# A scan's input products with their three precision parts stacked along the contraction, and its matrices laid out on the host

## The chip, the cores and the metric

The kernel runs on one core of one Trainium2 chip. The time is device microseconds of that core, from runs of the compiled program; a profiled execution of the same program gives the trace. TensorE (PE, with its weight loads as PEld), VectorE (DVE), ScalarE (ACT) and GpSimd (POOL) each take their instructions in program order and wait for each other through semaphores; SP's queue and POOL's queue issue the DMA transfers.

## The reference, cut to what matters

One decoder layer for 304 tokens (16 meta, 256 prompt, 32 sample): a SwiGLU block, a mixer and a second SwiGLU block, in float32. The mixer projects its input to a pooled branch, a state-space branch and two gates. The state-space branch is the part that is changed:

```python
b_bar = ((lam_bar - 1.0) / lam)[..., None] * b_mat          # (64 groups, 64 states, 16 channels), complex
ug = u.astype(f32).reshape(nb, L, N_SSM_GROUPS, SSM_GS)     # 64 groups of 16 channels
bu = jnp.einsum('blgc,gpc->blgp', ug.astype(jnp.complex64), b_bar)
...
_, h = lax.associative_scan(combine, (a, bu), axis=1)       # h[t] = lam_bar * h[t-1] + bu[t]
y = jnp.einsum('blgp,gcp->blgc', h, c_mat).real
```

So each group of 16 channels is multiplied by its own 64 x 16 complex matrix, the states run along the tokens, and each group is multiplied back.

## The kernel before, in words

**Projections.** Channels lie on partitions, tokens along the free dimension. A weight comes in chunks of 4 x 128 rows by 256 columns (512 KB), loaded by SP's queue three chunks deep. Every float32 product is made of three float32r ones: ACT rounds the chunk to its high part (`whi`, line 158), DVE makes the rest (`wlo`, line 167), and `mm3` (lines 245 to 247) multiplies high by high, high by low and low by high into one PSUM bank: 24 matmuls per chunk. `whi` and `wlo` have four buffers each. `step` (after each chunk) sets the order of all the rest: it casts the chunk three ahead, runs what the last projection left to do (`g.post`), makes the low part, starts a load, and then advances a side generator by `g.rate` turns; a turn is what lies between two `yield`s. `SETRATE` is 1.25 turns per chunk while the scan's tables are made, `MIXRATE` 2.25 while the scan runs. Nothing is reordered later: an instruction that waits holds back all that follows it on its engine.

**The setup** (`ssm_setup`, side work of the first SwiGLU block) makes the scan's tables. Of it the change touches the input matrices: b (states on partitions) is multiplied by two tables of coefficients `cr` and `ci` (lines 785 to 793) into the real part, the imaginary part and their sum, `bx[0..2]`; for each of 8 blocks `spread` copies the pieces into a block-diagonal tile (ACT), PE transposes it three times (`bt`, line 831), ACT and DVE split it into high and low part (`bc`, lines 832 and 833), and POOL's queue writes it to DRAM (`bsc`, line 835).

**The scan** (`Scan`) goes through 8 blocks of 128 channels. A block has four quads of 32 channels (two groups each), and each quad gives 128 state rows. `parted` (lines 877 and 878) splits the block's input `u` into `uhi` and `ulo`. `into`, once for each `ri` (sum, imaginary, real), multiplies: four quads times three part products, 12 matmuls of 32 contraction rows each (line 888), where the quads lie on different partitions; ACT copies the four banks into `row` tiles (line 892). Then `rows` turns half a block at a time (two quads, 12 turns): products with the tables `ee`, subtractions, two first-order scans (line 924), products back, and the states (line 943). `outof` (line 903) multiplies the rows by the c matrices, three turns into the next block. POOL's queue loads `ee` (line 860), the b matrices `bs` (line 867) and the c matrices `cs` (line 870).

**Around it.** While the scan runs, PE does the rest of the mixer's projections: the last part of the input projection, the pooled branch's map (`pw`, two chunks, each split into `Y` by ACT and DVE, line 274, which also frees its PSUM bank), then gates and branch products (`pj`). The main PSUM pool has four banks, the auxiliary one three, and one bank is apart.

Of the kernel before, what the change touches and what calls it, by code (L numbers as in the profile page):

```python
# [18 lines left out]
P = 128  # L19
# [22 lines left out]
NJ = 32  # L42
JB = 2
NA = S0 // 16
NTV = 16 + NA
POOLRATE = 3.5
LATE = 8
STIR = 9
LAG = 2
ROWS = 15  # L50
MAGIC = 12582912.0
# [6 lines left out]
def host_consts():  # L58
    import numpy as np

    c = np.zeros((P, NT + NTV), np.float32)
    c[:, :NT] = 1.0
    c[:, 0] = 0.0
    c[:, S0:NT:NS] = 0.0
    c[:, NT:NT + 16] = np.arange(16)
    c[:, NT + 16:NT + NTV] = 16 * np.arange(NA)
    return {"consts": c}

# [132 lines left out]
def tables(g):  # L201
    g.ident = g.const.tile([P, P], F32, name="ident")
    make_identity(g.nc, g.ident)
    g.hc = g.const.tile([P, NT + NTV], F32, name="hc")
    g.nc.gpsimd.dma_start(g.hc, g.I["consts"])
# [50 lines left out]
def bank(g, name, aux=False, pool=None):  # L256
    return (pool or (g.psaux if aux else g.psum)).tile([P, 512], F32, tag="ps", name=nm(g, name))
# [337 lines left out]
def ssm_setup(g):  # L595
# [7 lines left out]
    g.esc = [g.dram.tile([P, 3, JB, NT], F32, name=f"esc{b}") for b in range(NJ // JB)]  # L603
    g.bsc = [g.dram.tile([P, 2, 3, P], F32R, name=f"bsc{i}") for i in range(KW)]
    g.csc = g.dram.tile([KW, P, 3 * P], F32, name="csc")
    tv = g.hc[:, NT:NT + NTV]

    with ExitStack() as cs_:
# [172 lines left out]

        bc = lambda t: t.unsqueeze(2).to_broadcast(SB)
# [25 lines left out]

        bds = [T(f"bd{k}", [P, 3, 4, 2, 16]) for k in range(2)]
        for bd in bds:  # L810
            nc.gpsimd.memset(bd, 0.0)
            yield 1

        def spread(m):

            for i in range(3):
                for a in range(2):
                    rows = slice(a * 64, (a + 1) * 64)
                    nc.scalar.copy(bds[m % 2][rows, i, :, a], bx[i][rows, m * 4:(m + 1) * 4])

        spread(0)
        yield 1
        for m in range(KW):
            bc = sp.tile([P, 2, 3 * P], F32R, name=nm(g, "bc"), tag="bc", bufs=2)
            if m + 1 < KW:
                spread(m + 1)
                yield 1
            ps = bank(g, "bt", aux=True)
            for i in range(3):
                src = bds[m % 2][:, i].rearrange("p j a c -> p (j a c)")  # L830
                nc.tensor.transpose(ps[:, i * P:(i + 1) * P], src, g.ident)  # L831
            nc.scalar.copy(bc[:, 0], ps[:, :3 * P])
            tt(bc[:, 1], ps[:, :3 * P], bc[:, 0].bitcast(F32), ALU.subtract)
            yield 1
            nc.gpsimd.dma_start(g.bsc[m].rearrange("p h i s -> p h (i s)"), bc)


class Scan:
# [24 lines left out]
    def matrices(self, i, ins=True, outs=True):  # L863
        g = self.g
        if ins:
            self.bs[i] = self.sp.tile([P, 2, 3, P], F32R, tag="bs", name=nm(g, "bs"), bufs=1)
            g.nc.gpsimd.dma_start(self.bs[i], g.bsc[i])
        if outs:
            self.cs[i] = self.sp.tile([P, 3, P], F32, tag="cs", name=nm(g, "cs"), bufs=2)
            g.nc.gpsimd.dma_start(self.cs[i].rearrange("p i s -> p (i s)"), g.csc[i])  # L870

    def parted(self, i):

        g, nc = self.g, self.g.nc
# [3 lines left out]
        nc.vector.tensor_tensor(lo, self.u[i], hi.bitcast(F32), ALU.subtract)  # L878
        self.up = hi, lo

    def into(self, i, pair, ri):

        g = self.g
        pss = [bank(g, "bu", aux=True, pool=g.pslong if q == 3 else None)[:, :NT] for q in range(4)]
        for n, (b, u) in enumerate(((0, 0), (0, 1), (1, 0))):
            for q, ps in enumerate(pss):
                rows = slice(q * 32, (q + 1) * 32)
                g.nc.tensor.matmul(ps, self.bs[i][rows, b, ri], self.up[u][rows], start=n == 0, stop=n == 2)  # L888
        for s in pair:
            s["bu"][ri] = self.tile("row", ROWS)  # L890
        for q, ps in enumerate(pss):
            g.nc.scalar.copy(pair[q // JB]["bu"][ri][:, q % JB], ps)

# [26 lines left out]
    def rows(self, sb, s):  # L920
# [455 lines left out]
```

## Time and profile before

| | |
|---|---|
| median of 3 runs | 2339.84 us (2339.74 to 2339.84) |
| span of the profiled execution | 2338.1 us, so 1.7 us of the time lie around it |
| PE busy | 2324.2 us (99%) |
| DVE, ACT, POOL busy | 1582.7, 977.4, 91.2 us (68%, 42%, 4%) |
| records of the input products (line 888) | 288, first at 976.2, last at 1255.7 us |
| records of the b transposes (line 831) | 24 |

A row of the timeline gives the start and the length in us, the engine, the line, the operation, the tile written and the tiles read, the shape, and in brackets the idle time before it and who ended it. Matmuls overlap: the length of one says little, the distance from its start to the next one's start is what PE spends. A DMA row gives the KB of one transfer and the median us from issue to landing.

### The profile page before, as it was taken

The numbers are of one execution on the slowest core, as the hardware profiler recorded it, in microseconds if no ns is written. First come the engines' busy times: TensorE is split into PE (matmuls) and PEld (weight loads), VectorE is DVE, ScalarE is ACT, GpSimd is POOL, SyncE is SP. The second block draws the span as 40 slices with busy tenths as digits, with TensorE's granted clock in tenths as the row PEclk, the third lists the DMA queues.
The fourth block names the chain that finished last, engine by engine and source line by source line (L and its number), as shares of the span: only waits on it lengthen the run. The fifth ranks groups of instructions, "written<-read, shape, count | busy, mean of one in ns | idle before, by whom it ended". The sixth has DMA issues, their size and how long they took to land.

```text
span 2338.1 us, 42307 instructions
## 1 busy us (share of the span) xinstructions
PE 2324.2 (99%) x17391; PEld 2306.1 (99%) x17391; DVE 1582.7 (68%) x2415; ACT 977.4 (42%) x1432; POOL 91.2 (4%) x166
## 2 busy tenths in 40 slices
PE   9999999999999999999999999999999999999998
PEld 9999999999999999999999999999999999999997
DVE  7788777877554558699999765545555555555655
ACT  6333433333533335455455544333333333333334
POOL 0000000001000002000000130000000000000000
PEclk9999999999999999999999999999999999999999
DMA  6445556556654446556666674454444555455553
GB/s 224 160 153 192 196 202 210 197 192 200 221 167 158 158 159 221 184 191 231 225 237 211 206 264 163 163 169 165 164 170 163 168 166 166 163 167 167 167 164 112
DMA packets 119857, 429.95 MB, mean 184 GB/s; under 512 B 14644, under 2 KB 20032, under 8 KB 119656
## 3 DMA queue, kind: packets, MB, share of 16 engines
q1 hardware_dynamic: 106944, 374.35, 48.0%
q0 software_dynamic: 12432, 52.71, 6.7%
q8 instruction: 136, 2.23, 0.4%
q14 instruction: 57, 0.47, 0.1%
q10 hardware_dynamic: 288, 0.19, 0.0%
HBM read 397.61 MB, written 29.95 MB: 183 GB/s over the span
## 4 chain that ended last, share of the span: by engine, by line
PE 98%; DMA 1%; DVE 1%; ACT 0%; issue 0%; ACTq 0%; DVEq 0%
PE pj L245 24%; PE pj L246 24%; PE pj L247 24%; PE dn L247 8%; PE dn L245 8%; PE dn L246 8%; PE bu L888 1%; PE yps L903 1%; DMA raw<-in_ffn_w_gate 0%; DMA raw<-in_ffn_w_up 0%; DVE acc L334 0%; DMA vec<-in_vec 0%; PE bt L831 0%; PE ss L344 0%; ACT y L1264 0%
## 5 line engine op out<-in xcount | busy, mean ns | idle before, releaser
L167 DVE TENSOR_TENSOR wlo<-raw,whi 128x1024 fp32r<-128x1024 f32 x695 | 848.9, 1222 | 568.6 <-ACT whi L158 562.9
L158 ACT CAST whi<-raw 128x1024 fp32r<-128x1024 f32 x695 | 729.7, 1051 | 1139.2 <-PE pj L246 690.6
L245 PE MATMUL pj<-X,whi 128*128 128x304 f32 (+1 forms) x2432 | 733.0, 301 | 0.7 <-DVE Y L274 0.5
L246 PE MATMUL pj<-X,whi 128*128 128x304 f32 (+1 forms) x2432 | 729.7, 300 | 0.0
L247 PE MATMUL pj<-X,wlo 128*128 128x304 f32 (+1 forms) x2432 | 729.2, 300 | 0.5 <-DVE wlo L167 0.5
L246 PE MATMUL pj<-Y,whi 128*128 128x288 f32 x1728 | 510.2, 295 | 0.0
L245 PE MATMUL pj<-Y,whi 128*128 128x288 f32 x1728 | 509.9, 295 | 0.0
L247 PE MATMUL pj<-Y,wlo 128*128 128x288 f32 x1728 | 509.3, 295 | 0.0
L245 PEld LDWEIGHTS pj<-X,whi 128*128 128x128 f32 x2432 | 458.3, 188 | 7.0 <-issue 5.1
L247 PEld LDWEIGHTS pj<-X,wlo 128*128 128x128 f32 x2432 | 457.6, 188 | 1.0 <-DVE wlo L167 0.8
L246 PEld LDWEIGHTS pj<-X,whi 128*128 128x128 f32 x2432 | 457.8, 188 | 0.0
L245 PEld LDWEIGHTS pj<-Y,whi 128*128 128x128 f32 x1728 | 325.2, 188 | 2.1 <-issue 2.0
L246 PEld LDWEIGHTS pj<-Y,whi 128*128 128x128 f32 x1728 | 325.0, 188 | 0.0
L247 PEld LDWEIGHTS pj<-Y,wlo 128*128 128x128 f32 x1728 | 324.5, 188 | 0.0
L247 PE MATMUL dn<-H,wlo 128*128 128x304 f32 x704 | 213.0, 303 | 0.0
L245 PE MATMUL dn<-H,whi 128*128 128x304 f32 x704 | 213.0, 303 | 0.0
L246 PE MATMUL dn<-H,whi 128*128 128x304 f32 x704 | 212.2, 301 | 0.0
L246 PE MATMUL dn<-X,whi 128*128 128x288 f32 x704 | 207.7, 295 | 0.0
L245 PE MATMUL dn<-X,whi 128*128 128x288 f32 x704 | 207.5, 295 | 0.0
L247 PE MATMUL dn<-X,wlo 128*128 128x288 f32 x704 | 207.4, 295 | 0.0
L246 PEld LDWEIGHTS dn<-H,whi 128*128 128x128 f32 x704 | 132.4, 188 | 0.0
L246 PEld LDWEIGHTS dn<-X,whi 128*128 128x128 f32 x704 | 132.4, 188 | 0.0
(259 smaller groups left out, 1840.1 us busy)
## 6 DMA issues: line engine op xcount, KB each, us to landing
raw<-in_ffn_w_down SPq DMA_DIRECT2D x176, 512.0 KB, 3.5
raw<-in_ffn_w_gate SPq DMA_DIRECT2D x175, 512.0 KB, 3.5
raw<-in_ffn_w_up SPq DMA_DIRECT2D x175, 512.0 KB, 3.5
raw<-in_w_in SPq DMA_DIRECT2D x96, 512.0 KB, 4.0
raw<-in_w_out SPq DMA_DIRECT2D x32, 512.0 KB, 4.0
esc<-ee POOLq DMA_DIRECT2D x16, 912.0 KB, 5.9
ee<-esc POOLq DMA_DIRECT2D x16, 912.0 KB, 6.6
raw<-in_w_branch_a SPq DMA_DIRECT2D x16, 512.0 KB, 3.5
```

The costliest lines, as they stand in the source:

```text
L158: self.g.nc.scalar.copy(hi, self.raw[i])
L167: self.g.nc.vector.tensor_tensor(lo, raw, hi.bitcast(F32), ALU.subtract)
L245: mm(ps, wh, x[0], start=start, stop=False)
L246: mm(ps, wh, x[1], start=False, stop=False)
L247: mm(ps, wl, x[0], start=False, stop=stop)
L888: g.nc.tensor.matmul(ps, self.bs[i][rows, b, ri], self.up[u][rows], start=n == 0, stop=n == 2)
L903: g.nc.tensor.matmul(self.yps[i][q * 32:q * 32 + 32], c[:, h, q], s["k"][h][:, jj, NMETA:], start=k == 0, stop=k == 2)
```

## The change

**Parts stacked.** `parted` now writes `uhi` and `ulo` to DRAM (`usc`) and reads them back as a tile `us` of 96 partitions: rows 0 to 31 hold the high part, 32 to 63 the low part, 64 to 95 the high part again, with the four quads along the free dimension. The b matrices are kept likewise (`bs`, 96 rows: high, high, low; three loads in place of one). One matmul of 96 rows then sums the three part products of a quad, and `into` does two quads of one `ri` (a half) at a time: two matmuls and two copies.

**Matrices from the host.** b arrives with the channels of a quad on partitions, as (128, 8, 64). PE's transposes of it go. Its coefficients must now lie along the free dimension: PE transposes `cr` and `ci` (two matmuls), DVE copies them, and POOL's queue writes them to DRAM (`crs`) and reads them back, broadcast over 16 partitions at a time (`crb`, eight reads). The block-diagonal high and low parts come from ACT and DVE with a 0/1 column of the constants table as a factor, and go to `bsc` in sixteen writes.

**Placement.** The scan begins one chunk earlier (`LAG` 1); the first products come five turns behind the first `parted`. The matrices and parts of block i + 2 are asked for at turn 10 of the second half of block i; the products of block i + 1 come at turns 5, 8 and 11 of the first half of block i and at 2, 5 and 8 of the second. `rows` works in the product's own tiles, with 12 row buffers for 15.

```diff
-LAG = 2
-ROWS = 15
+LAG = 1
+ROWS = 12
...
+        ps = bank(g, "ct", aux=True)
+        for i, c in enumerate((cr, ci)):
+            nc.tensor.transpose(ps[:NJ, i * P:(i + 1) * P], c, g.ident)
+        ct = T("ct", [NJ, 2, P])
+        V.tensor_copy(ct.rearrange("j i s -> j (i s)"), ps[:NJ, :2 * P])
+        for a in range(2):
+            for i in range(2):
+                nc.gpsimd.dma_start(g.crs[:, a, i].rearrange("q m p -> m q p"), ct[:, i, a * 64:(a + 1) * 64])
+        crb = T("crb", [P, 2, KW, 64])
+        for q in range(4):
+            for a in range(2):
+                r0 = 32 * q + 16 * a
+                src = g.crs[q, a].rearrange("i m p -> (i m p)").unsqueeze(0).to_broadcast([16, 2 * KW * 64])
+                nc.gpsimd.dma_start(crb[r0:r0 + 16].rearrange("r i m p -> r (i m p)"), src)
...
-        tt(m1, bb[0], bc(cr), ALU.mult)
-        tt(m2, bb[1], bc(ci), ALU.mult)
+        tt(m1, bb[0], crb[:, 0], ALU.mult)
+        tt(m2, bb[1], crb[:, 1], ALU.mult)
...
+                nc.scalar.activation(h, bx[i], AF.Copy, scale=own)
+                yield 1
+                stt(l, bx[i], own, h.bitcast(F32), ALU.mult, ALU.subtract)
+                yield 1
         for m in range(KW):
-            ...
-            for i in range(3):
-                src = bds[m % 2][:, i].rearrange("p j a c -> p (j a c)")
-                nc.tensor.transpose(ps[:, i * P:(i + 1) * P], src, g.ident)
-            nc.scalar.copy(bc[:, 0], ps[:, :3 * P])
-            tt(bc[:, 1], ps[:, :3 * P], bc[:, 0].bitcast(F32), ALU.subtract)
-            yield 1
-            nc.gpsimd.dma_start(g.bsc[m].rearrange("p h i s -> p h (i s)"), bc)
+            for k, part_ in enumerate((hi, lo)):
+                nc.gpsimd.dma_start(g.bsc[m][k].rearrange("r q x -> q r x"), part_[:, m].rearrange("p i a s -> p (i a s)"))
+            yield 1
...
-            self.bs[i] = self.sp.tile([P, 2, 3, P], F32R, tag="bs", name=nm(g, "bs"), bufs=1)
-            g.nc.gpsimd.dma_start(self.bs[i], g.bsc[i])
+            bs = self.bs[i] = self.sp.tile([96, 4, 3 * P], F32R, tag="bs", name=nm(g, "bs"), bufs=1)
+            for n, k in enumerate((0, 0, 1)):
+                g.nc.gpsimd.dma_start(bs[32 * n:32 * n + 32], g.bsc[i][k])
...
-        self.up = hi, lo
+        self.up = self.sp.tile([96, 4, NT], F32R, tag="us", name=nm(g, "us"), bufs=1)
+        for k, u in enumerate((hi, lo)):
+            nc.gpsimd.dma_start(g.usc[i][k], u)
+        for n, k in enumerate((0, 1, 0)):
+            nc.gpsimd.dma_start(self.up[32 * n:32 * n + 32], g.usc[i][k].rearrange("(q r) t -> r q t", q=4))
...
-        pss = [bank(g, "bu", aux=True, pool=g.pslong if q == 3 else None)[:, :NT] for q in range(4)]
-        for n, (b, u) in enumerate(((0, 0), (0, 1), (1, 0))):
-            for q, ps in enumerate(pss):
-                rows = slice(q * 32, (q + 1) * 32)
-                g.nc.tensor.matmul(ps, self.bs[i][rows, b, ri], self.up[u][rows], start=n == 0, stop=n == 2)
+        row = pair[half]["bu"][ri] = self.tile("row", ROWS)
+        for jj in range(JB):
+            q = half * JB + jj
+            ps = bank(g, "bu", aux=True, pool=g.pslong if long and jj else None)[:, :NT]
+            g.nc.tensor.matmul(ps, self.bs[i][:, q, ri * P:(ri + 1) * P], self.up[:, q], start=True, stop=True)
+            g.nc.scalar.copy(row[:, jj], ps)
...
-        k1, k3, k2 = (self.tile("row", ROWS) for _ in range(3))
+        k1, k3, k2 = bs, bi, br
...
-                    if h == 0 and n == 2 and i + 1 < KW:
-                        self.matrices(i + 1, outs=False)
-                    if h == 0 and n == 4 and i + 1 < KW:
-                        self.parted(i + 1)
-                    if h and i + 1 < KW and n in (4, 7, 10):
-                        self.into(i + 1, nxt, {4: 2, 7: 1, 10: 0}[n])
+                    k, late = divmod(h * len(rows) + n - 5, 3)
+                    if i + 1 < KW and late == 0 and 0 <= k < 6:
+                        self.into(i + 1, nxt, 2 - k % 3, k // 3)
+                    if h and n == 10 and i + 2 < KW:
+                        self.matrices(i + 2, outs=False)
+                        self.parted(i + 2)
```

PE, before: one group of input products (the first of the scan, with the projection products around it).

```order
L247 MATMUL pj_10802<-X_9852,wlo_10789 128x304
L888 MATMUL bu_10903<-uhi_10899,bs_10304 128x304
L888 MATMUL bu_10904<-uhi_10899,bs_10304 128x304
L888 MATMUL bu_10905<-uhi_10899,bs_10304 128x304
L888 MATMUL bu_10906<-uhi_10899,bs_10304 128x304
L888 MATMUL bu_10903<-ulo_10900,bs_10304 128x304
...
L245 MATMUL pj_10801<-X_9898,whi_10827 128x304
```

PE, now: one pair of them (the first of block 1).

```order
L250 MATMUL pj_11073<-X_9596,wlo_10972 128x304
L897 MATMUL bu_11112<-us_11028,bs_11020 128x304
L897 MATMUL bu_11115<-us_11028,bs_11020 128x304
L248 MATMUL pj_11072<-X_9643,whi_11014 128x304
L249 MATMUL pj_11072<-X_9644,whi_11014 128x304
```

Where twelve matmuls stood in one place, two stand in each of six places, and each reads the tile `us` that comes from DRAM.

POOL's queue, before: its issues for blocks 1 and 2.

```order
L867 DMA bs_11135<-bsc_735 128x768
L870 DMA cs_11244<-csc 128x384
L860 DMA ee_11340<-esc_720 128x1824
L860 DMA ee_11601<-esc_721 128x1824
L867 DMA bs_11645<-bsc_736 128x768
```

POOL's queue, now, for the same blocks.

```order
L872 DMA bs_11020<-bsc_735 32x1536 x3
L886 DMA usc_743<-uhi_11024 128x304
L886 DMA usc_743<-ulo_11025 128x304
L888 DMA us_11028<-usc_743 32x4x304 x3
L875 DMA cs_11151<-csc 128x384
L864 DMA ee_11234<-esc_720 128x1824
L872 DMA bs_11466<-bsc_736 32x1536 x3
L886 DMA usc_744<-uhi_11470 128x304
L886 DMA usc_744<-ulo_11471 128x304
L888 DMA us_11474<-usc_744 32x4x304 x3
L864 DMA ee_11485<-esc_721 128x1824
```

The writes and reads of the parts stand between the b matrices and the next `ee`.

DVE, before: between the two chunks of the pooled branch's map (`pw`), with the scan's rows.

```order
L274 SCALAR_TENSOR_TENSOR Y_11327<-pw_11313,vec,Y_11326 128x288
L167 TENSOR_TENSOR wlo_11330<-raw_11207,whi_11320 128x1024
L950 TENSOR_TENSOR row_11337<-row_10920,ee_10897 128x608
L951 TENSOR_TENSOR row_11338<-row_11008,ee_10897 128x608
L274 SCALAR_TENSOR_TENSOR Y_11359<-pw_11344,vec,Y_11358 128x288
```

DVE, now, at the same place.

```order
L277 SCALAR_TENSOR_TENSOR Y_11284<-pw_11270,vec,Y_11283 128x288
L170 TENSOR_TENSOR wlo_11287<-raw_11147,whi_11277 128x1024
L957 TENSOR_TENSOR row_10939<-row_10939,ee_10820 128x608
L953 TENSOR_TENSOR row_10939<-row_10889,row_10939 128x608
L945 TENSOR_TENSOR row_10939<-row_10939,ah 128x2x8
L930 SCALAR_TENSOR_TENSOR row_10939<-d_1656_11231,row_10939 128x608
L277 SCALAR_TENSOR_TENSOR Y_11317<-pw_11302,vec,Y_11316 128x288
```

The rows run ahead of where they ran, so other ones (turns 1 to 3 of a half in place of 0 and 1) fall between the splits.

More of the change, by code (lines that the diff above doesn't have):

```diff
@@ L45 @@
 NTV = 16 + NA
+NCON = NT + NTV + 2
 POOLRATE = 3.5
@@ L59, in host_consts @@
     import numpy as np
-    c = np.zeros((P, NT + NTV), np.float32)
+    c = np.zeros((P, NCON), np.float32)
     c[:, :NT] = 1.0
@@ L66, in host_consts @@
     c[:, NT + 16:NT + NTV] = 16 * np.arange(NA)
+    for a in range(2):
+        c[:, NT + NTV + a] = np.arange(P) // 16 % 2 == a
     return {"consts": c}
@@ L203, in tables @@
     make_identity(g.nc, g.ident)
-    g.hc = g.const.tile([P, NT + NTV], F32, name="hc")
+    g.hc = g.const.tile([P, NCON], F32, name="hc")
     g.nc.gpsimd.dma_start(g.hc, g.I["consts"])
@@ L603, in ssm_setup @@
     g.esc = [g.dram.tile([P, 3, JB, NT], F32, name=f"esc{b}") for b in range(NJ // JB)]
-    g.bsc = [g.dram.tile([P, 2, 3, P], F32R, name=f"bsc{i}") for i in range(KW)]
+    g.bsc = [g.dram.tile([2, 32, 4, 3 * P], F32R, name=f"bsc{i}") for i in range(KW)]
+    g.usc = [g.dram.tile([2, P, NT], F32R, name=f"usc{i}") for i in range(KW)]
+    g.crs = g.dram.tile([4, 2, 2, KW, 64], F32, name="crs")
     g.csc = g.dram.tile([KW, P, 3 * P], F32, name="csc")
@@ L753, in ssm_setup @@
                 hrs.append(hr)
-        SB = [P, NJ, 16]
+        SB = [P, KW, 64]
         bb = [T(f"bb{i}", SB) for i in range(2)]
         for i, name in enumerate(("ssm_b_re", "ssm_b_im")):
-            nc.gpsimd.dma_start(bb[i], I[name][0].rearrange("(j a) p c -> (a p) j c", a=2))
+            nc.gpsimd.dma_start(bb[i], I[name])
+        ps = bank(g, "ct", aux=True)
[8 more added lines that the diff above has]
+        for q in range(4):
+            for a in range(2):
+                r0 = 32 * q + 16 * a
+                src = g.crs[q, a].rearrange("i m p -> (i m p)").unsqueeze(0).to_broadcast([16, 2 * KW * 64])
+                nc.gpsimd.dma_start(crb[r0:r0 + 16].rearrange("r i m p -> r (i m p)"), src)
         cs = [None] + [T(f"cs{i}", [P, KW, 4, 16]) for i in range(1, 3)]
@@ L780, in ssm_setup @@
         yield 1
-        bc = lambda t: t.unsqueeze(2).to_broadcast(SB)
         m1, m2 = T("q0", SB), T("q1", SB)
         bx = [T(f"q{i + 2}", SB) for i in range(3)]
-        tt(m1, bb[0], bc(cr), ALU.mult)
-        tt(m2, bb[1], bc(ci), ALU.mult)
+        tt(m1, bb[0], crb[:, 0], ALU.mult)
+        tt(m2, bb[1], crb[:, 1], ALU.mult)
         tt(bx[0], m1, m2, ALU.subtract)
         yield 1
-        tt(m1, bb[0], bc(ci), ALU.mult)
-        tt(m2, bb[1], bc(cr), ALU.mult)
+        tt(m1, bb[0], crb[:, 1], ALU.mult)
+        tt(m2, bb[1], crb[:, 0], ALU.mult)
         tt(bx[1], m1, m2, ALU.add)
@@ L807, in ssm_setup @@
         nc.gpsimd.dma_start(g.csc.rearrange("m p x -> p m x"), cx.rearrange("p m i q a c -> p m (i q a c)"))
-        bds = [T(f"bd{k}", [P, 3, 4, 2, 16]) for k in range(2)]
-        for bd in bds:
-            nc.gpsimd.memset(bd, 0.0)
-            yield 1
-        def spread(m):
-            for i in range(3):
[L817 to L821, printed above, removed]
-        yield 1
[L823 to L829, printed above, removed]
-                src = bds[m % 2][:, i].rearrange("p j a c -> p (j a c)")
[L831 to L835, printed above, removed]
+        hi, lo = (sp.tile([P, KW, 3, 2, 64], F32R, name=nm(g, x), tag=x) for x in ("bhi", "blo"))
+        for i in range(3):
+            for a in range(2):
+                own = g.hc[:, NT + NTV + a:NT + NTV + a + 1]
+                h, l = hi[:, :, i, a], lo[:, :, i, a]
+                nc.scalar.activation(h, bx[i], AF.Copy, scale=own)
+                yield 1
+                stt(l, bx[i], own, h.bitcast(F32), ALU.mult, ALU.subtract)
+                yield 1
+        for m in range(KW):
+            for k, part_ in enumerate((hi, lo)):
+                nc.gpsimd.dma_start(g.bsc[m][k].rearrange("r q x -> q r x"), part_[:, m].rearrange("p i a s -> p (i a s)"))
+            yield 1
 class Scan:
@@ L878, in parted, with into @@
         nc.vector.tensor_tensor(lo, self.u[i], hi.bitcast(F32), ALU.subtract)
-        self.up = hi, lo
-    def into(self, i, pair, ri):
-        g = self.g
-        pss = [bank(g, "bu", aux=True, pool=g.pslong if q == 3 else None)[:, :NT] for q in range(4)]
-        for n, (b, u) in enumerate(((0, 0), (0, 1), (1, 0))):
-            for q, ps in enumerate(pss):
-                rows = slice(q * 32, (q + 1) * 32)
[L888 to L892, printed above, removed]
+        self.up = self.sp.tile([96, 4, NT], F32R, tag="us", name=nm(g, "us"), bufs=1)
[3 more added lines that the diff above has]
+            nc.gpsimd.dma_start(self.up[32 * n:32 * n + 32], g.usc[i][k].rearrange("(q r) t -> r q t", q=4))
+    def into(self, i, pair, ri, half, long=False):
+        g = self.g
+        row = pair[half]["bu"][ri] = self.tile("row", ROWS)
[4 more added lines that the diff above has]
+            g.nc.scalar.copy(row[:, jj], ps)
     def outof(self, i, pair):
@@ L970, in run @@
         nb = NJ // JB
+        self.parted(0)
         pair = [self.nxt, self.load(1)]
-        self.parted(0)
-        yield 1
+        for _ in range(5):
+            yield 1
         for ri in (2, 1, 0):
-            self.into(0, pair, ri)
-            for _ in range(3):
+            for h in range(half):
+                self.into(0, pair, ri, h, h == half - 1)
+            for _ in range(2):
                 yield 1
+        self.matrices(1, outs=False)
+        self.parted(1)
         done, acts = None, None
@@ L1361 @@
     arrays["vec"] = np.ascontiguousarray(arrays["vec"])
+    for n in ("ssm_b_re", "ssm_b_im"):
+        b = a(n).reshape(KW, 4, 2, 64, 16).transpose(1, 2, 4, 0, 3)
+        arrays[n] = np.ascontiguousarray(b.reshape(P, KW, 64))
     for n in ("ssm_c_re", "ssm_c_im"):
```

## The prediction

> **What bounds the kernel now.** I read the page's busy shares first, then the table by stretches, then who waited on PE, then single stretches of the timeline.
>
> ```profile
> span 2338.1 us, 42307 instructions
> PE 2324.2 (99%) x17391; PEld 2306.1 (99%) x17391; DVE 1582.7 (68%) x2415; ACT 977.4 (42%) x1432; POOL 91.2 (4%) x166
> PEclk9999999999999999999999999999999999999999
> 1000.00:1100.00 100.00, 99.51 (x818) 94.56 (x817) 95.21 (x141) 51.52 (x92) 4.80 (x9) 1.00 0.61 212
> ```
>
> The last row is one stretch of the scan; its columns are PE, PEld, DVE, ACT and POOL busy, clock, DMA share and GB/s. TensorE is full and its clock is granted in full, so the time is what PE's matmuls take one after another, plus any hole. In the scan's stretch DVE is 95% busy: work that PE loses in this stage brings DVE nearer to being the bound. PE's own waits come to 3 us in all, and the one that lies in the scan (0.49, "<-DVE Y") is quoted below.
>
> **The input products.** The first of the 24 groups, and then a place where a 96-row matmul already stands between projection products:
>
> ```profile
> 975.80 0.30 PE L246 MATMUL pj<-X,whi 128*128 128x304 f32 x1
> 975.94 0.30 PE L247 MATMUL pj<-X,wlo 128*128 128x304 f32 x1
> 976.17 0.41 PE L888 MATMUL bu<-uhi,bs 32*128 32x304 f32 x4
> 976.41 0.31 PE L888 MATMUL bu<-ulo,bs 32*128 32x304 f32 x4
> 976.55 0.30 PE L888 MATMUL bu<-uhi,bs 32*128 32x304 f32 x4
> 976.79 0.41 PE L245 MATMUL pj<-X,whi 128*128 128x304 f32 x1
> 977.03 0.30 PE L246 MATMUL pj<-X,whi 128*128 128x304 f32 x1
> ```
>
> ```profile
> 62.22 0.30 PE L247 MATMUL pj<-X,wlo 128*128 128x304 f32 x1
> 62.36 0.25 PE L620 MATMUL pt<-ident,pr 96*128 96x96 f32 x1
> 62.39 0.39 PE L245 MATMUL pj<-X,whi 128*128 128x304 f32 x1
> 62.62 0.30 PE L246 MATMUL pj<-X,whi 128*128 128x304 f32 x1
> ```
>
> Durations overlap, so I count from start to start. A 304-column product follows the last one by 0.138 us (975.80 to 975.94). From 975.94 to 977.03 lie 1.09 us where two ordinary steps would be 0.276: the group costs 0.81. Its four-row-block products do run four at once (x4 in one row), yet the steps into and out of the small shape are 0.23 to 0.24 instead of 0.138. L888 has 288 records, which is 24 groups of 12: 24 x 0.81 = 19.4, and one group (at 1014.99, below) is followed by the half microsecond of waiting: 19.9 in all.
>
> The change makes 8 x 3 x 4 = 96 products of 96 rows and 304 columns. Does a 96-row operand keep the ordinary step? The nearest row is pt: the step into it is 0.14 (62.22 to 62.36), as between projections, with none of the 0.09 that the 32-row group pays on entry. The 0.23 behind it (62.39 to 62.62) stands behind 128-row transposes too (605.52 to 605.75, below), so it isn't the 96 rows. I price a product at 0.138, 96 x 0.138 = 13.3. Upper bound: every one of the 48 pairs pays what a 32-row group pays beyond its three steps, 0.81 - 3 x 0.138 = 0.40, which would add 19; lower bound: none below 0.138, since nothing of 304 columns is quicker. Taken: 13.3 - 19.9 = **-6.6**.
>
> [...]
>
> **The setup.** 24 transposes of the b blocks go; two transposes of the coefficient tables come.
>
> ```profile
> L831 PE MATMUL bt<-ident,bd 128*128 128x128 f32 x24 | 3.8, 272 | 0.0
> 605.13 0.30 PE L247 MATMUL dn<-H,wlo 128*128 128x304 f32 x1
> 605.28 0.49 PE L831 MATMUL bt<-ident,bd 128*128 128x128 f32 x3
> 605.52 0.39 PE L245 MATMUL dn<-H,whi 128*128 128x304 f32 x1
> 605.75 0.30 PE L246 MATMUL dn<-H,whi 128*128 128x304 f32 x1
> ```
>
> From 605.13 to 605.75 are 0.62 where two steps are 0.28: 0.33 per three, 8 x 0.33 = 2.65. The pair that comes costs at most two thirds of that, 0.22: **-2.4**. DVE and ACT do as many elements as before (six pieces of 512 columns for eight of 384), and no PE work waits for them here. The new chain (table to DRAM, broadcast back) is twelve issues on POOL of 0.56 (607.17, below) and two hops of at most 4.5: 16 us. Its first reader, the b products on DVE, comes 11 turns of the side work later, at 1.25 turns per weight chunk of 24 x 0.138 = 3.3 us: 29 us. If that cover were gone, DVE would stand, and PE's next low half with it, one for one.
>
> **The new hand-over.** Every input row block now goes to DRAM and comes back in three pieces before PE may multiply it. POOL issues three bs reads, the two writes, and, only when these have landed, the three reads; behind them wait cs and the next ee. The writes wait for ulo on DVE, and PE waits for the last read in program order, with all projection work behind it. I price the chain from the end of ulo:
>
> ```profile
> 606.32 0.56 DVE L833 TENSOR_TENSOR bc<-bt,bc 128x384 fp32r<-128x384 f32 x1 [1.99 <-ACT bc L832]
> 607.17 0.56 POOL L835 DMA_DIRECT2D bsc<-bc  x1 [13.52 <-DVE bc L833]
> bsc<-bc POOLq DMA_DIRECT2D x8, 384.0 KB, 2.7
> xsc<-xc POOLq DMA_DIRECT2D x16, 144.0 KB, 3.7
> zb<-gsc POOLq DMA_DIRECT2D x16, 144.0 KB, 3.5
> hist<-in_state_pool POOLq DMA_DIRECT2D x4, 120.0 KB, 4.5
> ```
>
> 0.3 from DVE's end (606.88) to the issue, 2.7 for the write to land, 0.55 for the issue of the reads' last one behind the other, 3.5 to 4.5 for it to land (152 KB each): **7.5** with 3.95. Low: 6.4 (both transfers at about the quick end, 2.5 and 3.0). High: 9.4 (3.7 for the write, 4.5 for the read, and 0.35 of wake-ups).
>
> Against it stands the time from ulo to its first product. I counted it from the program order, 24 projection products to a weight chunk. For three short ones, the DVE row behind which ulo will stand, ulo's length, and the PE row that the product will precede:
>
> ```profile
> 970.57 1.23 DVE L167 TENSOR_TENSOR wlo<-raw,whi 128x1024 fp32r<-128x1024 f32 x1 [1.03 <-ACT whi L158]
> 975.07 0.47 DVE L878 TENSOR_TENSOR ulo<-u,uhi 128x304 fp32r<-128x304 f32 x1
> 990.86 1.23 DVE L167 TENSOR_TENSOR wlo<-raw,whi 128x1024 fp32r<-128x1024 f32 x1 [2.95 <-ACT whi L158]
> 998.53 0.30 PE L245 MATMUL pj<-X,whi 128*128 128x304 f32 x1
> 1066.77 0.74 DVE L959 TENSOR_TENSOR row<-row,ee 128x576 f32<-128x576 f32 x1
> 1074.63 0.40 PE L245 MATMUL pj<-Y,whi 128*128 128x288 f32 x1
> ```
>
> Block 0: ulo would end at 972.2 (its turn comes 1.15 after a wlo starts), and its product stands one chunk (24 x 0.138 = 3.3) behind the chunk that starts at 976.1 once the old group is gone: 979.4, so 7.2 us. Block 1: 992.5 to 998.5, 6.0. Block 3: 1067.9 to 1074.6, 6.7. By the same count block 6 has 7.2 and blocks 2, 4, 5 and 7 have 8.6 to 9.4. With 7.5 for the chain PE waits 0.3 + 1.5 + 0.8 + 0.3 = **+2.9**. With 6.4 it waits 0.4; with 9.4 it waits 2.2 + 3.4 + 2.7 + 2.2 and 1.6 on the others, 12.1.
>
> **A place where DVE is late.** Rows now start one row earlier, so DVE has other scan work between the pool map's splits, and PE's next projection needs the bank which the first of the later splits frees:
>
> ```profile
> 1013.07 1.21 DVE L167 TENSOR_TENSOR wlo<-raw,whi 128x1024 fp32r<-128x1024 f32 x1
> 1014.20 0.78 DVE L950 TENSOR_TENSOR row<-row,ee 128x608 f32<-128x608 f32 x1
> 1015.60 1.78 DVE L274 SCALAR_TENSOR_TENSOR Y<-pw,vec,Y 128x288 fp32r<-128x288 f32 x4
> 997.79 1.42 DVE L924 TENSOR_TENSOR_SCAN row<-d,row 128x608 f32<-128x608 f32 x1
> 1014.99 0.41 PE L888 MATMUL bu<-uhi,bs 32*128 32x304 f32 x4
> 1016.17 0.40 PE L245 MATMUL pj<-X,whi 128*128 128x288 f32 x1 [0.49 <-DVE Y L274]
> ```
>
> Two row products (1.4 us) stand there before; then one product, a subtraction, a small addition and a scan: 0.7 + 0.8 + 0.15 + 1.3 = 2.95. The first split ends 1.55 later, near 1017.7, while PE, with two products of 0.138 where the group stands from 1014.9, is ready at about 1015.2: a wait of **+2.5**, whose old size (0.5) is in the 19.9 above. Low 0.5 if DVE catches up, high 3.
>
> **Sum:** -6.6 - 2.4 + 2.9 + 2.5 = -3.6, so the span is 2334.5; the runs' median is 1.7 above the profiled span, which gives 2336.2. Three things I cost at nothing. ACT's copies of the products keep their number and length. Fewer row buffers and rows written in place cost nothing because a buffer's last reader, the output product of the block before, is two turns ahead of its next writer; else ACT would wait for PE, and the weight casts behind it. The ee load is issued up to 7.5 us later, behind the reads:
>
> ```profile
> ee<-esc POOLq DMA_DIRECT2D x16, 912.0 KB, 6.6
> ```
>
> It has half a block, 12 turns at 2.25 per chunk, 17.6 us, to land in 6.6; without that slack DVE's rows would stand and wlo behind them.
>
> **Rivals.** (1) The hand-over is hidden: chain 6.4 or less. For it: half the blocks have 8.6 us or more, and a hole at one block lets DVE catch up before the next. Against it: no read row of this size lands under 3.5 at the median. -6.6 - 2.4 + 2.5 + 0.4 = -6.1: 2333.7. [...] (2) The hand-over decides: chain 9.4, because bs reads of 576 KB stand in the same queue ahead of it and the weight stream fills 61 to 64% of the DMA engines. -6.6 - 2.4 + 2.5 + 12.1 = +5.6: 2345.4; it turns slower than before from a chain of about 8.4. (3) The 96-row shape pays the toll of the small one, 48 x 0.2 to 0.4: +6 to +16, 2349; the pt row speaks against it.
>
> **How the numbers follow.** A time within 0.2% (4.7 us) is about what a measurement here cannot tell from no change. Forecast (part of the gain lost in two kinds of holes, between 2335.2 and 2340) 0.40; rival 1, with the neighbours that end below 2335.2, 0.39; rival 2 (chain over 8.4) 0.18, of which half stays under 4.7 us; rival 3 0.03. So faster 0.39, same 0.40 + 0.09 = 0.49, slower 0.09 + 0.03 = 0.12. The range runs from rival 1 with the pool wait small too (2332) to a chain of about 9.0 (2342.5); the forecast's own is 2335 to 2340.
>
> **What would show it.** Right: bu in 96 records with steps of 0.138 and no gap of 0.23 around them; PE waits of 1 us or so ending in DMA us at blocks 1 and 3; a wait near 2.5 us at the first gate projection on the split of pw. Wrong: no us wait at all (rival 1), us waits at most blocks (rival 2), 0.2 gaps around each pair (rival 3), or a new DVE wait on wlo through the whole scan, which none of the sums holds.

## The result, and the profile after

| | before | after |
|---|---|---|
| median | 2339.84 us (2339.74 to 2339.86, 4 runs) | 2359.58 us (2357.96 to 2363.74, 4 runs) |
| ratio, 95% interval | 1 | 1.0086 (1.0072 to 1.0100) |
| span of the profiled execution | 2338.1 us | 2358.6 us |

The kernel became 0.86% slower. The forecast was 2336.2 us with a range of 2332 to 2342.5, so it was wrong in sign and the time lies outside the range.

After, the head of the page:

```profile
span 2358.6 us, 41931 instructions
PE 2322.6 (98%) x17177; PEld 2310.0 (98%) x17177; DVE 1584.2 (67%) x2414; ACT 967.7 (41%) x1382; POOL 130.7 (6%) x240
```

The row of one stretch of the scan, columns as in the prediction:

```profile
1000.00:1100.00 100.00, 90.66 (x683) 87.62 (x682) 86.50 (x128) 48.66 (x87) 13.42 (x26) 0.98 0.65 210
```

PE's longest waits in the scan (us in total, times, longest):

```profile
PE bu L897 <- DMA us<-usc: 14.5, 7, 3.5
PE bu L897 <- DMA cs<-csc: 4.6, 1, 4.6
PE pj L248 <- DVE Y L277: 2.4, 1, 2.4
```

In that stretch PE falls from 99.5 to 90.7 us of 100 and DVE from 95.2 to 86.5: nothing else took PE's place, PE stood. It stood in front of the input products, at every one of the eight blocks. (The 4.6 put down to `cs` is block 1's wait for `us`: the `cs` load was issued last on that queue, and PE doesn't need it there.)

**Where the 20 us come from.** I took the start of the first product on each weight chunk in both traces, in program order, and subtracted. Before the setup's transposes the changed kernel is 0.5 us behind; at chunk 200 it is 1.7 us ahead, and it is still so at chunk 284 (964 us). At chunk 368 it is 20.0 us behind, and from there on it changes by 0.3 at most. So the setup gave 2.2, and the scan took 21.7. The steps from start to start between 966 and 1345 us account for the scan:

| term | us |
|---|---|
| 288 products of 32 rows (19.8 with their steps in and out) become 96 of 96 rows (13.25 at the ordinary step) | -6.6 |
| gap before the first gate projection (split of the pooled map), 2.73 for one step | +2.6 |
| eight gaps before a block's first input product, 21.4 for eight steps | +20.3 |
| each block's second product, 0.24 for 0.14 | +0.8 |
| projection products behind three of the gaps, at half the clock | +4.3 |
| sum | +21.4 |

0.3 us stay unassigned. One hand-over, that of block 1, in the timeline: DVE, then POOL's queue, then PE.

```profile
993.44 0.47 DVE L883 TENSOR_TENSOR ulo<-u,uhi 128x304 fp32r<-128x304 f32 x1
```

```profile
990.63 1.49 POOL L872 DMA_DIRECT2D bs<-bsc  x3 [14.12 <-PE bu L897]
992.90 0.56 POOL L886 DMA_DIRECT2D usc<-uhi  x1 [0.79 <-ACT uhi L882]
994.21 0.54 POOL L886 DMA_DIRECT2D usc<-ulo  x1 [0.75 <-DVE ulo L883]
998.03 0.56 POOL L888 DMA_DIRECT2D us<-usc  x1 [3.28 <-DMA usc<-uhi]
999.69 1.09 POOL L888 DMA_DIRECT2D us<-usc  x2 [1.10 <-DMA usc<-ulo]
1000.76 0.57 POOL L875 DMA_DIRECT2D cs<-csc  x1
```

```profile
1000.04 0.30 PE L250 MATMUL pj<-X,wlo 128*128 128x304 f32 x1
1004.93 0.52 PE L897 MATMUL bu<-us,bs 96*128 96x304 f32 x2 [4.58 <-DMA cs<-csc]
1005.28 0.41 PE L248 MATMUL pj<-X,whi 128*128 128x304 f32 x1
1005.49 0.46 PE L249 MATMUL pj<-X,whi 128*128 128x304 f32 x1
1005.74 0.46 PE L250 MATMUL pj<-X,wlo 128*128 128x304 f32 x1
```

`ulo` ends at 993.9, its write is issued 0.3 later, the read that waits for it 5.5 after that (hop 1), the last read 0.54 behind, and PE starts 4.7 after that (hop 2): 11.0 us, where the prediction had 7.5 for the chain and 6.0 for the window. Over the eight blocks hop 1 is 4.0 to 5.5 (mean 4.66), hop 2 3.7 to 6.9 (5.31), the chain 9.7 to 12.1 (10.84). A block's chain less its wait gives the window that it really had: 8.4 us at blocks 3 and 6, where the prediction counted 6.7 and 7.2, and 6.3 to 9.4 at the others, within 0.3 of the count. With the counted windows these chains ask for about 24 us of waiting; the trace has 20.3. The windows were nearly right, the chain was not.

The DMA issues between 965 and 1290 us, before and after (transfers, KB of each, median us to landing), show what such transfers took beside the scan:

```profile
raw<-in_w_in SPq DMA_DIRECT2D x71, 512.0 KB, 3.8
bs<-bsc POOLq DMA_DIRECT2D x7, 384.0 KB, 7.8
msc<-z SPq DMA_DIRECT2D x16, 144.0 KB, 2.8
cs<-csc POOLq DMA_DIRECT2D x7, 192.0 KB, 5.2
```

```profile
raw<-in_w_in SPq DMA_DIRECT2D x66, 512.0 KB, 4.6
bs<-bsc POOLq DMA_DIRECT2D x21, 192.0 KB, 3.9
us<-usc POOLq DMA_DIRECT2D x24, 152.0 KB, 4.5
msc<-z SPq DMA_DIRECT2D x16, 144.0 KB, 3.5
cs<-csc POOLq DMA_DIRECT2D x7, 192.0 KB, 7.7
usc<-uhi POOLq DMA_DIRECT2D x8, 152.0 KB, 5.1
usc<-ulo POOLq DMA_DIRECT2D x8, 152.0 KB, 4.1
```

The trace of before held this stage's own rows: `cs` with 192 KB took 5.2 there and `bs` with 384 KB 7.8. The prediction used `bsc`, 384 KB in 2.7, from the setup, and reads from other stages. Not every row of this stage would have warned it: the sixteen writes `msc` of 144 KB, on SP's queue, have a median of 2.8 before, but single ones took 1.7 to 7.9 us.

### The profile page after: what moved, and what is told of

Read it like the earlier page. It is cut to its first block, busy times and chain, and to the rows that moved or that the text cites. A ratio compares the mean times of both kernels' runs of the same rounds, so it can differ in the third digit from the quotient of the medians.

```text
span 2358.6 us, 41931 instructions
## 1 busy us (share of the span) xinstructions
PE 2322.6 (98%) x17177; PEld 2310.0 (98%) x17177; DVE 1584.2 (67%) x2414; ACT 967.7 (41%) x1382; POOL 130.7 (6%) x240
## 4 chain that ended last, share of the span: by engine, by line
PE 93%; DMA 4%; issue 1%; DVE 1%; POOL 1%; ACT 0%; SPq 0%; ACTq 0%; POOLq 0%; DVEq 0%
PE pj L249 22%; PE pj L248 22%; PE pj L250 22%; PE dn L250 8%; PE dn L249 8%; PE dn L248 8%; DMA us<-usc 2%; DMA usc<-ulo 1%; PE bu L897 1%; DMA raw<-in_ffn_w_gate 0%; POOL bs L872 0%; DVE wlo L170 0%; DMA cs<-csc 0%; POOL us L888 0%; DMA raw<-in_ffn_w_up 0%
```

## The experiments

Theory **H**: PE waits for the parts' round trip through DRAM. Rivals: **D**, DVE with less slack is the bound; and inside H, what makes the trip long: **Q**, the b loads ahead on POOL's queue; **B**, the `ee` load behind; **S**, the size of the pieces; **P**, POOL's queue itself. In all of them the kernel before ran at 2339.8 to 2340.0 beside the variant.

**1. The hand-over for one block only.** Left out: the parts of blocks 1 to 7 are not made or moved; their products use those of block 0.

```diff
-        self.parted(1)
...
-                        self.parted(i + 2)
```

> The changed kernel, but the stacked input parts are made and moved for block 0 only; the products of blocks 1 to 7 read block 0's parts again (so the scan's outputs are of other inputs, and seven ACT casts, seven DVE subtractions and 35 transfers are left out). Theory H (the hand-over: in the changed kernel PE stands 21.2 us before the first products of the eight blocks, because the two DMA hops take about 10.8 us and not 7.5): the seven later holes (18.7 us) go, block 0's 2.5 and the pool map's 2.4 stay, the time is 2339 to 2342. Rival D (DVE, 94% busy, would hold PE anyway once these holes are gone): holes on wlo take their place and the time stays above 2347.

Measured: 2339.16 (2337.50 to 2341.21, 10 runs), 0.9998 (0.9988 to 1.0007), span 2335.6. PE's waits in the scan:

```profile
PE pj L248 <- DVE Y L277: 2.4, 1, 2.4
PE bu L897 <- DMA us<-usc: 2.2, 1, 2.2
```

Seven gaps are gone with seven hand-overs, and the one that is left is block 0's. D falls: with the holes away, DVE keeps up. (Seven subtractions of 0.47 us are gone from DVE too; run 2 has them.) The hand-over is worth the 20 us.

**2. The same transfers, with more time.** The products of the next block come at turns 11, 13, ... 21 of the two halves, in place of 5, 8, ... 20.

```diff
-                    k, late = divmod(h * len(rows) + n - 5, 3)
+                    k, late = divmod(h * len(rows) + n - 11, 2)
```

> The changed kernel with the products of the next block at turns 11, 13, ... 21 in place of 5, 8, ... 20; everything is computed. The parts are asked for at the same place, so each hand-over has six turns (8 to 9 us) more. Theory H: the holes of blocks 1 to 7 go, block 0's 2.5 us stays; time 2339 to 2342, like e1_once. Rival D: DVE's rows or wlo come late instead, time above 2347. Rival C (the transfers themselves take PE's time by contention, wherever the products stand): time stays within 5 us of the changed kernel's 2359.6.

Measured: 2341.42 (2339.73 to 2345.09, 10 runs), 1.0007 (0.9998 to 1.0017), span 2339.6. The gaps of blocks 1 to 7 are gone although every byte still goes through DRAM. In their place, in the list of PE's waits:

```profile
PE bu L897 <- ACT row L898: 3.2, 5, 1.8
```

With two turns from pair to pair, two pairs sometimes fall together, and four products need four banks where the auxiliary pool has three: PE waits for ACT's copy.

**3. Q: the b loads ahead taken away.** Left out: the b matrices are loaded for block 0 alone and used for all.

```diff
+            if i:
+                self.bs[i] = self.bs[0]
+            else:
...
```

> The changed kernel with the b matrices of block 0 loaded once and used for all blocks (outputs of the scan are of other matrices; 21 loads of 192 KB are left out). Theory Q (the three b loads, 576 KB ahead of the parts in the same queue, are what makes the chain 10.8 us long in place of 7.5): the chain falls to 7.5 to 8.5, the eight holes from 21.2 to 3 to 7 us, time 2342 to 2346. Theory I (two hops in a stream that fills 60% of the DMA engines take that long by themselves): chain 9.5 to 11, time 2355 to 2360.

Measured: 2355.10 (2354.76 to 2356.74, 4 runs), 1.0067 (1.0052 to 1.0082). The chain is 10.26 on the mean (hop 1 4.34, hop 2 5.08). Q carries 4.5 us of the 20; the trip is long without it.

**4. The scan begun where it began before.**

```diff
-LAG = 1
+LAG = 2
```

> The changed kernel with the scan begun a chunk later, as before the change (LAG 2). My theory of the pool map's wait (DVE does turns 1 to 3 of a half between the splits in place of 0 and 1): the wait of PE on the split Y falls from 2.4 to about 0.5, time 1 to 3 us less, if the hand-overs stay as they are; the hand-over holes still come to 17 to 24 us. Rival: the wait on Y comes from the holes before it and stays above 1.5.

Measured: 2359.68 (2356.24 to 2361.24, 4 runs), 1.0083 (1.0068 to 1.0098). The wait for `Y` went from 2.7 to 0.3, as the prediction's reason for it says, but the time stayed: block 1's gap grew from 4.9 to 6.9, and the granted clock was 0.50 for 17 us of the scan in place of 10 (the second cost below).

**5. More time and a fourth bank.** Run 2, with every second pair's second product in the bank that is apart.

```diff
-                        self.into(i + 1, nxt, 2 - k % 3, k // 3)
+                        self.into(i + 1, nxt, 2 - k % 3, k // 3, k % 2 == 1)
```

> e2_later, with the second product of every other pair in the PSUM bank that stands apart (as the first block's products have it), so that four products in one chunk find four banks. In e2_later PE stood 3.2 us on ACT's copies (five clusters of four products, three banks). If that is the cause, these waits go and the time is 2 to 4 us under e2_later's 2341.4: 2337.5 to 2339.5. If ACT itself is late, the wait moves to the bank that is apart and the time stays within 1 us.

Measured: 2337.47 (2335.31 to 2341.57, 10 runs), 0.9991 (0.9982 to 1.0000), span 2335.4. ACT's wait is gone; block 0's (1.6) and the pooled map's (2.2) stay.

**6. Run 5, with the scan a chunk earlier and eight turns for block 0.**

```diff
-LAG = 1
+LAG = 0
...
-        for _ in range(5):
+        for _ in range(8):
```

> e5_banks, with the scan begun one more chunk earlier (LAG 0) and eight turns in place of five between the first parts and the first products, so that block 0's hand-over has about 3.3 us more; everything is computed. Theory H: block 0's hole of 2.5 us goes as the others did, and of the pool map's wait (2.7) some 1.4 remain because the scan operation no longer stands between the splits (a product, a subtraction and an addition do). 3 to 4 us under e5_banks: 2334 to 2336, faster than before the change. Rival: block 0's hole stays because the input itself comes late; then within 1.5 us of e5_banks.

Measured: 2340.50 (2337.84 to 2344.47, 11 runs), 1.0004 (0.9995 to 1.0013). A miss. Up to chunk 374 it is 5.9 us ahead of the kernel before; then it loses 6.9. The last block's output products now fall behind the last paced chunk and wait for their rows, one after the other, and for 6.8 us behind these waits PE's products come 0.24 apart where an ordinary step is 0.13, which costs about 2.4 of the 6.9 (PE's waits):

```profile
PE yps L909 <- DVE row L964: 1.8, 1, 1.8
PE yps L909 <- DVE row L966: 1.1, 1, 1.1
```

**7. S: larger pieces for the reads.** `usc` is laid out by the reading side, so that a read takes 4864 bytes in one piece; the write is then scattered.

```diff
-    g.usc = [g.dram.tile([2, P, NT], F32R, name=f"usc{i}") for i in range(KW)]
+    g.usc = [g.dram.tile([2, 32, 4, NT], F32R, name=f"usc{i}") for i in range(KW)]
```

> The changed kernel with the parts laid in DRAM so that each of the 32 rows is read back in one piece of 4864 B and not four of 1216 B (the writes stay 128 pieces of 1216 B); everything is computed. Theory S (the number of pieces makes the reads slow): the chain from the end of ulo to the product falls from 10.8 to 9.3 or less, the eight holes from 21 to under 12 us, time 2346 to 2351. Theory I (latency of two hops under the weight stream): chain 10 to 11, time 2357 to 2361.

Measured: 2379.84 (2377.80 to 2388.78, 4 runs), 1.0177 (1.0161 to 1.0194). The DMA issues of the scan's stretch:

```profile
us<-usc POOLq DMA_DIRECT2D x24, 152.0 KB, 4.7
usc<-uhi POOLq DMA_DIRECT2D x8, 152.0 KB, 7.0
usc<-ulo POOLq DMA_DIRECT2D x8, 152.0 KB, 6.2
```

The reads are no quicker with a quarter of the pieces, and the writes, the same bytes in the same number of pieces but in another order in DRAM, take 2 us more. S falls for the reads.

**8. B: the `ee` loads behind taken away.** Left out: the tables are loaded for the first two half blocks alone and used for all.

```diff
+        if sb > 1:
+            return dict(ee=self.ees[sb % 2], bu={})
```

> The changed kernel with the tables ee of the first two half blocks used for all (the scan's outputs are of other tables; 14 loads of 912 KB, which stand in the queue right behind the reads of the parts, are left out). Theory B (these 912 KB share the DMA engines with the last reads and stretch them): the landing of us falls from 4.5 to about 3.5 us at the median, the chain from 10.8 to 9.5 or less, the holes from 21 to 10 to 14, time 2348 to 2353. Theory I: landings of 4.3 to 4.6, time 2356 to 2361.

Measured: 2360.79 (2356.51 to 2365.38, 4 runs), 1.0089 (1.0074 to 1.0103). Fourteen transfers of 912 KB are gone, and the chain is 11.2; `us` in the DMA issues of the same stretch:

```profile
us<-usc POOLq DMA_DIRECT2D x24, 152.0 KB, 5.2
```

B falls.

**9. P: the writes on SP's queue.**

```diff
-            nc.gpsimd.dma_start(g.usc[i][k], u)
+            nc.sync.dma_start(g.usc[i][k].bitcast(F32), u.bitcast(F32))
```

> The changed kernel with the two writes of the parts (usc) issued on SP's queue, as plain float32, in place of POOL's; the reads stay on POOL's. Theory P (the write is slow because POOL's queue carries it, behind the b loads): it lands as the 144 KB rows of SP's queue in this stage do (msc 2.8 to 3.5), hop 1 falls from 4.7 to about 3.2, the chain from 10.8 to 9.3, and against windows of 6.0 to 9.4 the holes fall from 21 to about 12 us: 2350. Theory S (the write is slow because the weight stream and the ee tables share the DMA engines): hop 1 stays at 4.3 to 5, the holes at 19 to 24, the time at 2357 to 2362. Against both: SP now waits for ulo in the row of weight loads; if that makes a weight late, a wait on raw shows on ACT or DVE and the time goes above 2362.

Measured: 2371.80 (2370.00 to 2373.59, 4 runs), 1.0139 (1.0123 to 1.0155). The writes in the DMA issues of the scan's stretch:

```profile
usc<-uhi SPq DMA_DIRECT2D x8, 152.0 KB, 5.2
usc<-ulo SPq DMA_DIRECT2D x8, 152.0 KB, 4.5
```

The write takes as long from SP's queue, and hop 1 (5.2) is longer than in the changed kernel (4.66); the chain is 11.9 on the mean and the eight gaps come to 30.2 us, where they were 21.4. P falls for the write.

**10. Run 6 with seven turns.**

```diff
-        for _ in range(8):
+        for _ in range(7):
```

> The kernel with later products and the long bank (two-turn spacing from turn 11), with the scan begun one chunk earlier still (LAG 0) and the first products seven turns behind the first parted, in place of eight. With eight turns it was 6.0 us ahead of the kernel before at chunk 374 and lost 6.8 behind it, where the last output products fell into the side work that nothing paces. If that is the loss, with seven turns the last output products come one chunk earlier, before that stretch, and most of the 6 us stay: 2334 to 2335. If the loss is rather DVE, which has the scan's last rows to do whatever the order is, it stays: 2338 to 2341. Block 0 has one turn less for its chain of about 11 us: a hole of up to 2.5 there in both.

Measured: 2336.72 (2335.11 to 2341.73, 11 runs), 0.9989 (0.9980 to 0.9997), span 2334.9. The last output products are back among paced chunks and the loss at the end is 0.8 in place of 6.9; PE's waits in the scan are 2.0 (`Y`), 0.9 (`us`) and 0.3. It is 2 us above what was expected of it.

**11 and 12. No DRAM: the engines write `us` themselves.** Eight copies on ACT and four subtractions on DVE, 32 rows each, that move rows between partitions; the placing is that of the changed kernel. Run 12 is the same with `LAG` 2.

```diff
+        for q in range(4):
+            own = slice(32 * q, 32 * q + 32)
+            nc.vector.tensor_tensor(self.up[32:64, q], self.u[i][own], hi[own].bitcast(F32), ALU.subtract)
+            for n in (0, 2):
+                nc.scalar.copy(self.up[32 * n:32 * n + 32, q], self.u[i][own])
```

> The changed kernel with the hand-over kept on the chip: us is written by the engines, quad by quad (eight copies on ACT, four subtractions on DVE, which move rows between partitions as they write), and nothing goes to DRAM and back. Everything else, the placing of the products too, as in the changed kernel. If the round trip through DRAM is the cause, the chain becomes 0.44 for uhi and 3.5 for ACT's eight copies, about 4 us against windows of 6.0 to 9.4: no hole at any block, the wait on the pooled map's split of 2.7 stays: -6.6 - 2.2 + 2.2 from 2339.8, so 2333 to 2336. If something else in the 96-row products' place makes the holes, they stay at about 20 and the time at 2355 to 2360. Rival: DVE does 1.4 us more per block (four operations of 0.47 for one), 11 us in a stretch where it has 14 to spare; if that makes it the bound, waits on wlo show through the scan and the time is 2338 to 2345.

> The same with the scan begun where it began before (LAG 2). In the changed kernel that took the wait on the pooled map's split from 2.7 to 0.3 but lost it again in a longer hole at block 1. With no holes to lose it in, it should be kept: about 2.4 less than the run without it, 2331 to 2334. If DVE is the bound here, nothing is gained, and the last output products come a chunk later, behind which the changed kernel's early variants lost 3 us and more: 2336 to 2342.

Measured: 2349.17 (2348.51 to 2351.67, 4 runs), 1.0043 (1.0027 to 1.0059), and 2350.00 (2349.68 to 2352.24, 5 runs), 1.0045 (1.0032 to 1.0058). No wait for `us` is left, but run 11 has another one in PE's list, and at its longest (1161 to 1166 us) this in ACT's timeline:

```profile
PE bu L896 <- ACT row L897: 6.6, 3, 5.1
```

```profile
1164.37 0.44 ACT L916 ACTIVATE gw<-gy 128x288 f32<-128x288 f32 x1 [6.05 <-DVE gy L915]
1165.75 0.71 ACT L897 COPY row<-bu 128x304 f32<-128x304 f32 x2
```

DVE, busy 4.93 of these 5 us (96.2 of the 100 from 1000 on), is late with `gy`; ACT stands for it, with the copy of the input products queued behind, and PE needs that copy's bank. So in this form D comes true: 11 us more on DVE are not there to be had. Both times lie in none of the ranges that were given for them, and the wait came by `gy` and not by `wlo`.

**13 and 14. No DRAM, and DVE's work as it was.** One `ulo` for all rows on DVE, and twelve copies of 32 rows on ACT; run 14 with `LAG` 2.

```diff
+            for n in (0, 2):
+                nc.scalar.copy(self.up[32 * n:32 * n + 32, q], self.u[i][own])
+        for q in range(4):
+            nc.scalar.copy(self.up[32:64, q], lo[32 * q:32 * q + 32].bitcast(F32))
```

> The changed kernel with the hand-over on the chip again, now with DVE's work as in the changed kernel: one ulo for all rows on DVE, and twelve copies of 32 rows on ACT (0.44 each, 5.3 per block) that put the parts into us. The chain is about 5 us from the end of ulo, under every window. If the round trip is the whole loss and DVE's 11 us were what the last pair of runs lost, then no hole is left but the wait on the pooled map's split (2.7, of which 0.5 is old): -6.6 - 2.2 + 2.2, a span of 2331 to 2334 and a median of 2333 to 2336. Rival: ACT, held for 5.3 us at a stretch, is late with its casts and copies; then waits on ACT whi or ACT row show and the median is 2338 or more.

> The same with the scan begun where it began before (LAG 2): the wait on the pooled map's split falls to about 0.3, and what the scan's end costs decides. 2331 to 2334 if the end stays covered; as the run without this, or above, if the last output products come a chunk later than is covered.

Measured: 2359.20 (2357.89 to 2360.46, 5 runs), 1.0084 (1.0071 to 1.0098), and 2360.08 (2359.42 to 2361.65, 4 runs), 1.0088 (1.0074 to 1.0102). A miss for the forecast, a hit for its rival. PE's longest waits in run 13:

```profile
PE bu L899 <- ACT row L900: 11.3, 5, 5.6
PE pw L248 <- DVE u L858: 3.3, 1, 3.3
```

Again no wait for `us`. The longest one, 5.6 us, begins with ACT: behind its copies into `us` the next weight cast comes late, and DVE stands for it (first row). DVE is then late with `gy`, ACT stands for that (second row), and the `row` copy that PE needs is queued behind:

```profile
1160.06 1.23 DVE L170 TENSOR_TENSOR wlo<-raw,whi 128x1024 fp32r<-128x1024 f32 x1 [5.25 <-ACT whi L161]
1172.02 0.44 ACT L919 ACTIVATE gw<-gy 128x288 f32<-128x288 f32 x1 [6.19 <-DVE gy L918]
```

So ACT, 60% busy in this stage, can't give 5.3 us at a stretch here. Whether the same copies, spread over several turns, would do was not tried, nor a transfer straight from tile to tile, with one hop in place of two.

## Why the prediction was wrong

**What held.** The bound: PE's matmuls one after another plus holes. The input products: 96 records, 0.14 apart, and no 0.23 step at either side of a pair where nothing waited:

```profile
1020.78 0.30 PE L897 MATMUL bu<-us,bs 96*128 96x304 f32 x1
1020.92 0.30 PE L248 MATMUL pw<-Y,whi 128*128 128x288 f32 x1
1021.05 0.30 PE L249 MATMUL pw<-Y,whi 128*128 128x288 f32 x1
```

-6.6 was right, and rival 3 (the toll) is out. The setup: -2.4 foreseen, -2.2 found. The pooled map's split: a wait of 2.5 foreseen, 2.4 by the list of waits and 2.6 by the steps, and run 4 shows its cause. The three things costed at nothing were nothing in the changed kernel: no wait of an input product on ACT, none on a row buffer, none of DVE on `ee`. Six of the eight windows fit the gaps within 0.3 us; two were 1.2 and 1.7 longer than counted.

**What failed is one term: the chain of the hand-over, 7.5 us, measured 10.84.** The write was priced at 2.7 and takes 4.66 to the issue of the read; the read at 3.95 and takes 5.31 to PE's start. That is 3.3 us on a chain that stood within 1.5 of every short window and 2 of every long one, so it didn't cost 3.3 once but at all eight blocks: 20.3 in place of 2.9. Even the high end, 9.4 with 12.1 us of waiting, was too low, and the range stopped at a chain of 9.0. Rival 2 named the right mechanism (slower from a chain of 8.4, by the prediction's own windows), and had 0.18. Its reason, the b loads ahead, is worth 4.5 us by run 3; its other reason, the weight stream, was not varied.

The error was in the choice of rows. The prediction took the quick row, the largest write, and gave no reason for it; that write ran in the setup, at 607 to 643 us. The rows of POOL's queue in the scan's own stretch (`cs` 5.2, `bs` 7.8) were in the same trace, and two hops of 4.5 to 5 with 0.85 for the issues give 10 to 11. That is hindsight: `msc` in the same stretch, 2.8, spoke for a quick write, and only run 9 shows that this write takes 4.5 to 5.2 on SP's queue too.

**A second cost stood in no sum.** Behind three of the eight gaps, 2.59, 4.88 and 3.76 us long (blocks 0, 1 and 4), PE's products come 0.24 to 0.25 apart for 3.4 us. Behind those of 2.79 and 2.70 (blocks 5 and 7) they don't. The granted clock is the last column but two; the stretches behind the gaps of blocks 0, 1, 4, 5 and 7, in this order:

```profile
981.45:984.86 3.41, 3.41 (x16) 3.41 (x15) 1.23 (x1) 1.45 (x3) 0.00 (x0) 0.50 0.15 61
1005.34:1008.75 3.41, 3.41 (x15) 3.41 (x14) 1.71 (x2) 1.67 (x3) 0.00 (x0) 0.50 0.00 0
1128.22:1131.63 3.41, 3.41 (x14) 3.41 (x15) 1.08 (x1) 1.67 (x3) 0.00 (x0) 0.50 0.56 227
1171.32:1174.50 3.18, 3.18 (x26) 3.18 (x25) 1.41 (x2) 1.67 (x3) 0.00 (x0) 1.00 0.71 289
1249.30:1252.40 3.10, 3.10 (x26) 3.10 (x25) 1.33 (x2) 1.68 (x3) 0.00 (x0) 1.00 0.57 227
```

The three stretches at 0.50 cost 4.3 us together; the last section sets two gaps of other runs beside these. A range that reaches to gaps of 3 us should hold this too.

**What is settled and what isn't.** Settled: the gaps are waits for the parts' trip through DRAM (run 1 removes them with the transfers, runs 2, 5 and 10 with time alone), and neither the b loads (beyond 4.5 us), nor `ee`, nor the reads' piece size, nor the issuing queue of the write makes the trip long. Open: why a transfer of 152 KB takes 4 to 5 us in this stage. In the traces it went with what else was moving: between 965 and 1290 us of all sixteen traces, the 144 KB writes of SP's queue (`msc` and another like it, `gsc`) landed in 1.8 us at the median where neither a weight nor an `ee` load was on its way at their issue (53 of them), in 2.7 beside a weight load (230), and in 5.2 beside both (143). For the parts, run 8 found no gain without `ee`, so the weight stream is the suspect left; no run varied it, and PE's work can't be had without it. Open too is why runs of one variant scatter by 2 to 11 us, where those of the kernel before, all but one, lie within 1.5 of those beside them. Part of it goes with the clock: the shortest of run 7 had a mean granted clock of 0.992 and the longest, 11 us above it, 0.988. Why it differed between them no run shows.

## What to carry to other kernels

Price a transfer from rows of the stage and the queue in which it will run, and look at single ones besides the median: POOL's queue landed 384 KB in 2.7 us in the setup and 192 KB in 5.2 beside the scan. When a hand-over goes through DRAM, add up issue, landing, issue and landing, compare with the time to the first reader at each place, and ask what one or two us more would cost at all of them together; if the answer is larger than the gain, place the reader later first: here six turns and one more bank turned 1.0086 into 0.9991 (0.9982 to 1.0000), so the loss was gone, with little or no gain behind it. Here an engine that was 95% busy couldn't take the work over either, and one that was 60% busy not in one piece.

## What the runs showed of the hardware

- The length of PE's gap alone didn't tell whether the granted clock fell behind it. It was 0.50 behind gaps of 2.42 us (run 4, block 3; first row) and of 2.59 (block 0 of the changed kernel, above), and 1.00 behind gaps of 2.79 (block 5, above) and of 3.45 (run 9, block 7; second row). What decided it was not shown.

```profile
1086.50:1088.00 1.50, 1.50 (x7) 1.50 (x8) 0.25 (x2) 0.98 (x3) 0.00 (x0) 0.50 0.94 364
```

```profile
1258.00:1259.00 1.00, 1.00 (x9) 1.00 (x9) 0.00 (x0) 0.79 (x3) 0.00 (x0) 1.00 1.01 412
```

- The order of the pieces in DRAM mattered for the write: the same 152 KB in pieces of 1216 bytes landed in 4.1 to 5.1 us laid out by partition, and in 6.2 to 7.0 interleaved (run 7), while the reads did not gain from pieces four times as long (4.5 and 4.7).
- The 32-row operations took as long as the 128-row ones: on DVE the subtraction of run 11 (466 ns) as that of the changed kernel above (0.47 us), and on ACT the copies of run 11 (443 ns) as `uhi` before (440). Splitting one operation by quads made four of the same length.

```profile
L885 DVE TENSOR_TENSOR us<-u,uhi x32: 464/466/470, 970.1 to 1228.2; 32x304 fp32r<-32x304 f32 x32
L887 ACT CAST us<-u x64: 439/443/449, 969.1 to 1226.4; 32x304 fp32r<-32x304 f32 x64
```

```profile
L877 ACT CAST uhi<-u x8: 436/440/442, 973.8 to 1224.3; 128x304 fp32r<-128x304 f32 x8
```
